# Column sums by zero-and-one matrices in a hybrid decoder layer: fp32 products replaced by pairs of fp32r products

## Chip, cores and metric

One core of one Trainium2 chip. The metric is the device time of one execution in microseconds; given are the median of three runs and one profiled execution, from which all views of the trace come. Engines: PE is TensorE (PEld its weight load), DVE is VectorE, ACT is ScalarE, POOL is GpSimd, SP is the engine that issues most DMAs.

## What is computed

A decoder layer over 2048 tokens and 1024 columns. The input projection feeds two mixers that run side by side: four HGRN2 heads of 128 columns and eight RWKV-7 heads of 64 columns. The output projection, a feed-forward block with a causal convolution, and a last norm follow. Cut to what matters here:

```python
h = _rmsnorm(x, norm1_w[l]);  proj = h @ w_in[l]
# HGRN2: o from a gated recurrence, then a norm over the 128 columns of a head
o = o * lax.rsqrt(jnp.mean(o * o, axis=-1, keepdims=True) + NORM_EPS)
# RWKV-7, heads of 64 columns
kk = heads(k * k_k)
kk = kk / jnp.maximum(jnp.sqrt(jnp.sum(kk * kk, axis=-1, keepdims=True)), L2_EPS)
y = _rwkv7_scan(heads(r), heads(decay), heads(k), heads(v), -kk, kk * heads(a))
var = jnp.mean(jnp.square(y - mu), axis=-1, keepdims=True)
y = ((y - mu) * lax.rsqrt(var + RW_GN_EPS)).reshape(B, T, RW_WIDTH)
bonus = jnp.sum(heads(r * k * r_k), axis=-1, keepdims=True) * heads(v)
```

The four sums over a head's columns (of `o * o`, `kk * kk`, `(y - mu)^2` and `r * k * r_k`) are what the change touches.

## The kernel before

Activations stand with their columns on the 128 partitions and 512 tokens (a block) on the free axis. A sum over the columns of a head is then a sum over partitions, and the kernel makes it on PE with a 128x128 matrix of zeros and ones: `ones`, all ones, for a head of 128 columns; `blk1`, two 64x64 squares of ones, for a pair of 64-column heads. Each such product also spreads the sum over the head's partitions.

The first stage (`phase1`, until about 1430 us) runs three generators. `dense` makes the projections: it loads a slice of weights, splits it into two fp32r halves (an ACT cast into `wh`, line 243, and a DVE subtraction of the cast from the source into `wl`, line 244), and makes every product as three fp32r products (`mm3`, lines 259 to 261), accumulated in the banks `pj`. Behind the columns of a block it turns the next block's rows (`turn`, line 427: transposes by `ident`, evicted by ACT into `xt`). `rw_super` treats four RWKV heads (two pairs, `u` = 0 and 1) of one block: eight runs of it. `hg_unit` treats one HGRN2 head of one block: sixteen runs. Each `yield` ends a step; a driver takes one step of each mixer and then fills 2 us of estimated TensorE time with projection work. Each engine runs its instructions in the order in which the scheduler put them, so that order is fixed before the kernel runs.

Four places make the sums, all as plain fp32 products. In `rw_super`: line 648 sums `sq`, a part of the tile `mk` (the squared keys); line 666 sums `BV` (r * k * r_k); line 886 sums `y1`, a part of `yo` (the squared outputs). Each makes two products of 128x512, one for each pair. In `hg_unit`, line 1016 sums `osq` in one product. The trace shows each product as two records. In the texts these are the sums of mk, of BV, of yo and of hg. The end of one `rw_super` (yo) and the beginning of the next (mk, BV, then the arrays AR and KB, and the first products of the chunk, line 687) stand close together; this stretch is called a boundary. Line 1022 and line 901 store the mixers' outputs, and the second stage begins with the last block's output projection.

The tiles with the tags `E` and `Ti` hold a triangular inverse (lines 749 to 767), solved by DVE in the middle of a run; before the solve, lines 750 and 751 clear `Ti` and set its diagonal.

Of the kernel before, what the change touches and what calls it, by code (L numbers as in the profile page):

```python
# [7 lines left out]
F32 = mybir.dt.float32  # L8
F32R = mybir.dt.float32r
# [3 lines left out]
ALU = mybir.AluOpType  # L13
# [5 lines left out]
P = 128  # L19
# [3 lines left out]
BLK = 512  # L23
# [6 lines left out]

C_CEN, C_ONE, C_S1, C_DG = 0, 128, 256, 384
C_LV = 448
C_SCAN = C_LV + 6 * 64
C_ID = C_SCAN + 512
C_W = C_ID + 128
# [26 lines left out]
def tile_layer(ctx, tc, consts, x, norm1_w, w_in, hg_lb_logits, hg_norm_w, rw_shift_mu, rw_w0, rw_w2,  # L62
# [17 lines left out]
    ident = cp.tile([P, P], F32, name="ident")  # L80
    cst = cp.tile([P, C_ID], F32, name="cst")
    dma(ident, consts[:, C_ID:C_ID + P])
# [3 lines left out]
    cen = cst[:, C_CEN:C_CEN + P]  # L86
    blk1 = cst[:, C_ONE:C_ONE + P]
    s1m = cst[:, C_S1:C_S1 + P]
    dgm = cst[:, C_DG:C_DG + 64]
    scanm = cst[:, C_SCAN:C_SCAN + 512]  # L90
    ones = cp.tile([P, P], F32, name="ones")
    V.memset(ones, 1.0)

# [3 lines left out]
    def eps_tile(v, name):  # L97
        t_ = cp.tile([P, 1], F32, name=name)
        V.memset(t_, v)
        return t_  # L100

    eps6 = eps_tile(1e-6, "eps6")
    epsgn = eps_tile(64e-5, "epsgn")

    tables = {AF.Exp: "natural_log_exp_and_others", AF.Ln: "natural_log_exp_and_others",
# [48 lines left out]
    def vec(nm, i):  # L154
        return vt[:, off[nm] + i:off[nm] + i + 1]
# [4 lines left out]
    lb1 = vt[:, off["lb"] + 4:off["lb"] + 8]  # L160
    ltmp = cp.tile([P, 16], F32, name="ltmp")
    V.tensor_max(ltmp[:, 0:4], lb0, lb1)
# [9 lines left out]
    V.tensor_scalar(omu, vt[:, off["mu"]:off["mu"] + 14], -1.0, 1.0, ALU.mult, ALU.add)  # L172
    oka = cp.tile([P, 16], F32, name="oka")[:, 0:4]
    V.tensor_scalar(oka, vt[:, off["ka"]:off["ka"] + 4], -1.0, 1.0, ALU.mult, ALU.add)
# [60 lines left out]
    def split_to(hi, lo, src):  # L235
        S.copy(hi, src)
        V.tensor_sub(lo, src, hi.bitcast(F32))
# [9 lines left out]
    def transposed(xt, nm, psum, evict):  # L247

        n = len(xt)
        for k in range(KD):  # L250
# [4 lines left out]
            yield 109 * n  # L255

    def mm3(acc, lhs, rhs, first, last, skip=False):
        (lh, ll), (rh, rl) = lhs, rhs
        TE.matmul(acc, lh, rh, start=first, stop=False, skip_group_check=skip)  # L259
        TE.matmul(acc, lh, rl, start=False, stop=False, skip_group_check=skip)  # L260
        TE.matmul(acc, ll, rh, start=False, stop=last, skip_group_check=skip)  # L261

    def phase1(c1):
# [7 lines left out]
        g2 = hp.tile([P, 512], F32, name="g2")  # L271
        lastc = hp.tile([P, 64], F32, name="lastc")
        nc.gpsimd.memset(lastc, 0.0)
        Xc = hp.tile([P, 4, 64], F32, name="Xc")
        nc.gpsimd.memset(Xc, 0.0)
# [205 lines left out]
        def constants():  # L481

            dma(w2a2[0:64, :], rw_w2[0])
            dma(w2a2[64:128, :], rw_a2[0])
            dma(cst, consts[:, 0:C_ID])
            dma(g2, rw_g2[0])
# [121 lines left out]
        U = range(2)  # L608

        def rw_super(nb, s_):  # L610
# [6 lines left out]
            def tile_(tag, shape, name):  # L617
                return rp.tile([P] + shape, F32, tag=tag, name=name)

            def bank2():  # L620
                return ps.tile([P, 2, BLK], F32, tag="rw", name="rw", bufs=2)
# [12 lines left out]
            mk_ = tile_("M", [4, 2, BLK], "mk")  # L634
            c, km, sq = mk_[:, 0], mk_[:, 1], mk_[:, 2]
            for u in U:
                V.tensor_tensor_scan(c[:, u], scanm, iW[:, u], 0.0, ALU.mult, ALU.add)
                act(sq[:, u], k[:, u], AF.Square, scale=vec("kk", prs[u]))
                act(km[:, u], a[:, u], AF.Identity, bias=oka[:, prs[u]:prs[u] + 1], scale=vec("ka", prs[u]))
            yield  # L640
            W = tile_("UV", [16, 65], "W")
            WC = tile_("WC", [16, 1], "WC")
            V.memset(W[:, :, 0:1], 1.0)
            act(W[:, :, 1:65], c16(c), AF.Exp, scale=NEG_C)
            act(iW, c, AF.Exp, scale=-NEG_C)
            b1 = bank2()
            for u in U:
                TE.matmul(b1[:, u, :], blk1, sq[:, u], start=True, stop=True)
            V.tensor_scalar_max(sq, b1, 1e-24)
# [9 lines left out]
            V.tensor_mul(RT, r4(r), W4[:, :, :, 1:65])  # L659
            yield  # L660
            BV = tile_("BV", [2, BLK], "BV")
            b1 = bank2()
            for u in U:
                V.scalar_tensor_tensor(BV[:, u], km[:, u], vec("rk", prs[u]), r[:, u], ALU.mult, ALU.mult)
            for u in U:
                TE.matmul(b1[:, u, :], blk1, BV[:, u], start=True, stop=True)
            for u in U:
# [213 lines left out]
            y1, y2 = yo[:, 0], yo[:, 1]  # L881
            act(y1, yp, AF.Square)
            yield
            b1 = bank2()
            for u in U:
                TE.matmul(b1[:, u, :], blk1, y1[:, u], start=True, stop=True)
            act(y1, b1, AF.Ln, bias=epsgn, scale=1.0 / 64)
# [18 lines left out]
        def hg_unit(nb, j):  # L906
# [105 lines left out]
            sq = rp.tile([P, BLK], F32, tag="hk", name="osq")  # L1012
            act(sq, op, AF.Square)
            yield
            ms = bank("hg")
            TE.matmul(ms, ones, sq, start=True, stop=True)
            act(sq, ms, AF.Ln, bias=eps6, scale=1.0 / 128)
# [471 lines left out]
```

## Time and profile before

| what | value |
|---|---|
| three runs, median (lowest to highest) | 2788.16 us (2784.22 to 2788.61) |
| profiled execution | 2785.02 us |
| its span, first to last instruction | 2783.2 us |
| mean granted TensorE clock | 0.984 |
| PE, DVE, ACT busy | 2678.8, 2066.4, 1421.1 us |
| DMA moved | 435.01 MB, mean 156 GB/s |

A row of a group names line, engine, operation, what it writes and reads, the shape and the count; then busy time and the mean of one in ns; then the idle time of the engine before it and what ended most of it. A row in order of time gives start, length and in brackets the idle time before. Matmuls are pipelined and their ends are modelled, so the records of neighbouring matmuls overlap: what one costs is seen from the distance of the starts.

### The profile page before, as it was taken

The numbers are of one execution on the slowest core, as the hardware profiler recorded it, in microseconds if no ns is written. First come the engines' busy times: TensorE is split into PE (matmuls) and PEld (weight loads), VectorE is DVE, ScalarE is ACT, GpSimd is POOL, SyncE is SP. The second block draws the span as 40 slices with busy tenths as digits, with TensorE's granted clock in tenths as the row PEclk, the third lists the DMA queues.
The fourth block names the chain that finished last, engine by engine and source line by source line (L and its number), as shares of the span: only waits on it lengthen the run. The fifth ranks groups of instructions, "written<-read, shape, count | busy, mean of one in ns | idle before, by whom it ended". The sixth has DMA issues, their size and how long they took to land.

```text
span 2783.2 us, 47784 instructions
## 1 busy us (share of the span) xinstructions
PE 2678.8 (96%) x18059; PEld 2135.2 (77%) x18059; DVE 2066.4 (74%) x3877; ACT 1421.1 (51%) x2254; POOL 11.1 (0%) x24
## 2 busy tenths in 40 slices
PE   8999999989999999999989999998999999999998
PEld 6877777767787777777767888886888888877887
DVE  4867778685686766868658789989997877677656
ACT  5445454544646446435346765456455555445444
POOL 0000000000000000000000000000000000000000
PEclk9999999999999999999899999999999999999999
DMA  5222322244441344543475457756672223998855
GB/s 163 72 69 72 99 73 78 63 131 141 131 121 58 102 141 136 161 132 94 131 239 178 143 172 262 239 165 216 205 245 88 87 76 135 324 333 310 289 193 186
DMA packets 429628, 435.01 MB, mean 156 GB/s; under 512 B 68703, under 2 KB 288213, under 8 KB 429397
## 3 DMA queue, kind: packets, MB, share of 16 engines
q1 hardware_dynamic: 428337, 429.30, 48.4%
q8 instruction: 142, 2.33, 0.3%
q0 software_dynamic: 992, 2.64, 0.2%
q14 instruction: 89, 0.73, 0.1%
q10 hardware_dynamic: 68, 0.02, 0.0%
HBM read 325.94 MB, written 105.91 MB: 155 GB/s over the span
## 4 chain that ended last, share of the span: by engine, by line
PE 78%; DVE 7%; ACT 7%; DMA 4%; issue 3%; SPq 1%; DVEq 0%; ACTq 0%
PE pj L259 8%; PE pj L260 8%; PE pj L261 8%; PE ua L261 6%; PE ua L259 5%; PE ua L260 5%; PE ud L259 3%; PE ud L260 3%; PE ud L261 3%; PE da L260 2%; PE da L261 2%; PE da L259 2%; PE hg L948 2%; PE db L259 2%; PE db L260 2%
## 5 line engine op out<-in xcount | busy, mean ns | idle before, releaser
L259 PE MATMUL pj<-hh,wh 128*128 128x512 f32 x960 | 401.8, 419 | 0.9 <-DVE xh L398 0.4
L260 PE MATMUL pj<-hl,wh 128*128 128x512 f32 x960 | 379.9, 396 | 0.0
L261 PE MATMUL pj<-hh,wl 128*128 128x512 f32 x960 | 379.0, 395 | 0.2 <-DVE wl L244 0.2
L243 ACT CAST wh<-wraw 128x512 fp32r<-128x512 f32 x240 | 147.0, 619 | 307.9 <-PE pj L260 266.2
L259 PE MATMUL ua<-Bh,uwh 128*128 128x512 f32 x704 | 278.6, 396 | 15.0 <-ACT uwh L243 13.7
L261 PE MATMUL ua<-Bh,uwl 128*128 128x512 f32 x704 | 276.6, 393 | 0.7 <-DVE uwl L244 0.7
L260 PE MATMUL ua<-Bl,uwh 128*128 128x512 f32 x704 | 276.5, 393 | 0.0
L244 DVE TENSOR_TENSOR wl<-wraw,wh 128x512 fp32r<-128x512 f32 x240 | 163.3, 686 | 133.8 <-ACT wh L243 132.9
L259 PEld LDWEIGHTS pj<-hh,wh 128*128 128x128 f32 x960 | 180.8, 188 | 53.1 <-issue 13.6
L260 PEld LDWEIGHTS pj<-hl,wh 128*128 128x128 f32 x960 | 180.9, 188 | 42.4 <-issue 7.9
L243 ACT CAST uwh<-uraw 128x512 fp32r<-128x512 f32 x220 | 134.9, 618 | 151.2 <-PE ua L260 80.0
L261 PEld LDWEIGHTS pj<-hh,wl 128*128 128x128 f32 x960 | 180.7, 188 | 39.9 <-issue 1.3
L243 ACT CAST dah<-draw 128x512 fp32r<-128x512 f32 x151 | 93.8, 621 | 182.7 <-PE da L260 50.5
L244 DVE TENSOR_TENSOR uwl<-uraw,uwh 128x512 fp32r<-128x512 f32 x220 | 146.9, 685 | 50.8 <-ACT uwh L243 50.8
L244 DVE TENSOR_TENSOR dal<-draw,dah 128x512 fp32r<-128x512 f32 x151 | 104.2, 690 | 107.0 <-ACT dah L243 106.8
L259 PEld LDWEIGHTS ua<-Bh,uwh 128*128 128x128 f32 x704 | 133.5, 190 | 44.0 <-ACT uwh L243 14.3
L261 PEld LDWEIGHTS ua<-Bh,uwl 128*128 128x128 f32 x704 | 133.6, 190 | 30.4 <-DVE uwl L244 2.3
L260 PEld LDWEIGHTS ua<-Bl,uwh 128*128 128x128 f32 x704 | 133.6, 190 | 27.2
L259 PE MATMUL ud<-Bh,uwh 128*128 128x512 f32 x352 | 137.9, 392 | 1.9 <-DVE cv L1340 1.9
L261 PE MATMUL ud<-Bh,uwl 128*128 128x512 f32 x352 | 137.1, 389 | 0.0
L260 PE MATMUL ud<-Bl,uwh 128*128 128x512 f32 x352 | 137.0, 389 | 0.0
L260 PE MATMUL da<-dbl,dah 128*128 128x512 f32 x340 | 133.5, 393 | 1.7 <-DVE dbl L244 1.6
(314 smaller groups left out, 5959.7 us busy)
## 6 DMA issues: line engine op xcount, KB each, us to landing
wraw<-in_w_in_dram SPq DMA_DIRECT2D x240, 256.0 KB, 3.0
uraw<-in_w_up_dram SPq DMA_DIRECT2D x176, 256.0 KB, 3.3
woraw<-in_w_out_dram SPq DMA_DIRECT2D x96, 256.0 KB, 3.1
draw<-Sg SPq DMA_DIRECT2D x88, 256.0 KB, 2.9
draw<-Tw SPq DMA_DIRECT2D x88, 256.0 KB, 3.0
gd<-y SPq DMA_DIRECT2D x86, 256.0 KB, 2.9
xt<-x1d SPq DMA_DIRECT2D x32, 512.0 KB, 6.6
draw<-gd SPq DMA_DIRECT2D x63, 256.0 KB, 5.1
```

The lines of the kernel that those rows point to most:

```text
L243: S.copy(hi, src)
L244: V.tensor_sub(lo, src, hi.bitcast(F32))
L259: TE.matmul(acc, lh, rh, start=first, stop=False, skip_group_check=skip)
L260: TE.matmul(acc, lh, rl, start=False, stop=False, skip_group_check=skip)
L261: TE.matmul(acc, ll, rh, start=False, stop=last, skip_group_check=skip)
L948: TE.matmul(o, kt[:, t0:t0 + 64], qs, start=True, stop=True, tile_position=(0, e * 64))
```

## The change

Every one of these fp32 products becomes two fp32r products. The source is split as the weights are: ACT casts it into an upper half (`hi`), DVE subtracts the cast from the source into a lower half (`lo`), and PE multiplies the zero-and-one matrix with each half and accumulates both in the same bank. The matrix itself becomes an fp32r tile. In `rw_super` both pairs are split by one cast and one subtraction of 1024 columns, one step before the products, so the four products of a sum stand together; the halves lie in the memory of the tags `E` and `Ti`. For that, the two DVE products that make `BV` move ahead of a `yield`. In `hg_unit` the halves are two tiles of the ring `hX`. `blk1` is loaded by a DMA of its own and cast by DVE; `ones` is made from `ident` by one DVE instruction. Some small tiles change their size or place.

```diff
-    blk1 = cst[:, C_ONE:C_ONE + P]
-    ones = cp.tile([P, P], F32, name="ones")
-    V.memset(ones, 1.0)
+    blk1, ones = (cp.tile([P, P], F32R, name=n_) for n_ in ("blk1", "ones"))
+    V.tensor_scalar(ones, ident, 0.0, 1.0, ALU.mult, ALU.add)
...
+    def mm_sum(accs, mat, his, los):
+        for acc, hi, lo in zip(accs, his, los):
+            TE.matmul(acc, mat, hi, start=True, stop=False)
+            TE.matmul(acc, mat, lo, start=False, stop=True)
...
-            dma(cst, consts[:, 0:C_ID])
+            dma(cst, consts[:, 0:C_ONE])
+            raw = wp.tile([P, P], F32, tag="wraw", name="blk", bufs=4)
+            dma(raw, consts[:, C_ONE:C_ONE + P])
+            V.tensor_copy(blk1, raw)
...
             c, km, sq = mk_[:, 0], mk_[:, 1], mk_[:, 2]
+            hi, lo = (rp.tile([P, 2, BLK], F32R, tag=t_, name="hl") for t_ in ("E", "Ti"))
             for u in U:
...
+            split_to(hi, lo, sq)
             yield
...
-            for u in U:
-                TE.matmul(b1[:, u, :], blk1, sq[:, u], start=True, stop=True)
+            mm_sum([b1[:, u, :] for u in U], blk1, [hi[:, u] for u in U], [lo[:, u] for u in U])
             V.tensor_scalar_max(sq, b1, 1e-24)
...
             V.tensor_mul(RT, r4(r), W4[:, :, :, 1:65])
-            yield
             BV = tile_("BV", [2, BLK], "BV")
+            for u in U:
+                V.scalar_tensor_tensor(BV[:, u], km[:, u], vec("rk", prs[u]), r[:, u], ALU.mult, ALU.mult)
+            split_to(hi, lo, BV)
+            yield
             b1 = bank2()
-            for u in U:
-                V.scalar_tensor_tensor(BV[:, u], km[:, u], vec("rk", prs[u]), r[:, u], ALU.mult, ALU.mult)
-            for u in U:
-                TE.matmul(b1[:, u, :], blk1, BV[:, u], start=True, stop=True)
+            mm_sum([b1[:, u, :] for u in U], blk1, [hi[:, u] for u in U], [lo[:, u] for u in U])
...
             act(y1, yp, AF.Square)
+            hi, lo = (rp.tile([P, 2, BLK], F32R, tag=t_, name="hl") for t_ in ("E", "Ti"))
+            split_to(hi, lo, y1)
             yield
             b1 = bank2()
-            for u in U:
-                TE.matmul(b1[:, u, :], blk1, y1[:, u], start=True, stop=True)
+            mm_sum([b1[:, u, :] for u in U], blk1, [hi[:, u] for u in U], [lo[:, u] for u in U])
...
             act(sq, op, AF.Square)
+            osp = [rp.tile([P, BLK], F32R, tag="hX", name="osp", bufs=3) for _ in range(2)]
+            split_to(*osp, sq)
             yield
             ms = bank("hg")
-            TE.matmul(ms, ones, sq, start=True, stop=True)
+            mm_sum([ms], ones, osp[:1], osp[1:])
```

Two places in the order of the instructions follow. Line numbers of the changed kernel are higher: its lines 236 and 237 are the cast and the subtraction of a split, 260 and 261 the two products of a sum, 265 to 267 the three products of a projection.

First boundary without transposes, PE around the sum of BV (`hl` is a half, `blk_76` the matrix), before:

```order
L261 MATMUL pj<-hh,wl 128x512
L666 MATMUL rw<-BV,cst 128x512 x2
L259 MATMUL pj<-hh,wh 128x512
L260 MATMUL pj<-hl,wh 128x512
L261 MATMUL pj<-hh,wl 128x512
```

and now:

```order
L267 MATMUL pj<-hh,wl 128x512
L260 MATMUL rw<-hl,blk_76 128x512
L265 MATMUL pj<-hh,wh 128x512
L266 MATMUL pj<-hl,wh 128x512
L267 MATMUL pj<-hh,wl 128x512
L265 MATMUL pj<-hh,wh 128x512
L261 MATMUL rw<-hl,blk_76 128x512
L260 MATMUL rw<-hl,blk_76 128x512
L261 MATMUL rw<-hl,blk_76 128x512
```

Between the sum of mk and that of BV stood 18 products of the projection; now 33 stand ahead of the first product of BV's upper half, and four more ahead of the lower half's. DVE at the same boundary, before, from BV on:

```order
L664 SCALAR_TENSOR_TENSOR BV<-mk,vt,rkv_358 128x512 x2
L654 COPY WC<-W 128x16
L659 TENSOR_TENSOR AR<-rkv_358,W 128x2x512
L649 TENSOR_SCALAR mk<-rw 128x1024
L672 TENSOR_TENSOR KB<-mk,ai 128x8x2x64
L333 SCALAR_TENSOR_TENSOR hq<-pj,sgm 128x512
L244 TENSOR_TENSOR wl<-wraw,wh 128x512 x2
L674 TENSOR_TENSOR ai<-ai 128x1024
```

and now:

```order
L672 SCALAR_TENSOR_TENSOR BV<-mk,vt,rkv_363 128x512 x2
L659 TENSOR_SCALAR mk<-rw 128x1024
L664 COPY WC<-W 128x16
L669 TENSOR_TENSOR AR<-rkv_363,W 128x2x512
L682 TENSOR_TENSOR KB<-mk,ai 128x8x2x64
L340 SCALAR_TENSOR_TENSOR hq<-pj,sgm 128x512
L244 TENSOR_TENSOR wl<-wraw,wh 128x512 x2
L684 TENSOR_TENSOR ai<-ai 128x1024
L237 TENSOR_TENSOR hl<-BV,hl 128x1024
L678 SCALAR_TENSOR_TENSOR mk<-rkv_446,vt,mk 128x512 x2
```

BV is made at the same place; its lower half stands eight instructions behind it.

First boundary with transposes, ACT (`xt` are the evictions of the transposes), before:

```order
L117 ACTIVATE hf<-pj 128x512
L113 ACT_TABLE_LOAD
L117 ACTIVATE mk<-mk 128x1024
L117 ACTIVATE xt<-pj 128x4x128
L117 ACTIVATE mk<-mk 128x1024
L117 ACTIVATE xt<-pj 128x4x128 x2
L243 CAST wh<-wraw 128x512
```

and now:

```order
L118 ACTIVATE hf<-pj 128x512
L114 ACT_TABLE_LOAD
L118 ACTIVATE mk<-mk 128x1024
L236 CAST hl<-BV 128x1024
L118 ACTIVATE mk<-mk 128x1024
L118 ACTIVATE xt<-pj 128x4x128 x2
L243 CAST wh<-wraw 128x512
```

The cast of BV stands ahead of the first eviction, which itself moved behind the second mk row.

More of the change, by code (lines that the diff above doesn't have):

```diff
@@ L29 @@
 HG_SCALE = 128.0 ** -0.5
-C_CEN, C_ONE, C_S1, C_DG = 0, 128, 256, 384
-C_LV = 448
+C_CEN, C_S1, C_DG = 0, 128, 256
+C_LV = 320
 C_SCAN = C_LV + 6 * 64
-C_ID = C_SCAN + 512
+C_ONE = C_SCAN + 512
+C_ID = C_ONE + 128
 C_W = C_ID + 128
@@ L80, in tile_layer @@
     ident = cp.tile([P, P], F32, name="ident")
-    cst = cp.tile([P, C_ID], F32, name="cst")
+    cst = cp.tile([P, C_ONE], F32, name="cst")
     dma(ident, consts[:, C_ID:C_ID + P])
@@ L103, in tile_layer @@
     epsgn = eps_tile(64e-5, "epsgn")
+    ltmp = cp.tile([P, 16], F32, name="ltmp")
+    blk1, ones = (cp.tile([P, P], F32R, name=n_) for n_ in ("blk1", "ones"))
+    V.tensor_scalar(ones, ident, 0.0, 1.0, ALU.mult, ALU.add)
     tables = {AF.Exp: "natural_log_exp_and_others", AF.Ln: "natural_log_exp_and_others",
@@ L160, in tile_layer @@
     lb1 = vt[:, off["lb"] + 4:off["lb"] + 8]
-    ltmp = cp.tile([P, 16], F32, name="ltmp")
     V.tensor_max(ltmp[:, 0:4], lb0, lb1)
@@ L172, in tile_layer @@
     V.tensor_scalar(omu, vt[:, off["mu"]:off["mu"] + 14], -1.0, 1.0, ALU.mult, ALU.add)
-    oka = cp.tile([P, 16], F32, name="oka")[:, 0:4]
+    oka = cp.tile([P, 32], F32, name="oka")[:, 0:4]
     V.tensor_scalar(oka, vt[:, off["ka"]:off["ka"] + 4], -1.0, 1.0, ALU.mult, ALU.add)
@@ L271, in phase1 @@
         g2 = hp.tile([P, 512], F32, name="g2")
-        lastc = hp.tile([P, 64], F32, name="lastc")
+        lastc, WC = (hp.tile([P, 32], F32, name=n_) for n_ in ("lastc", "WC"))
         nc.gpsimd.memset(lastc, 0.0)
+        WC = WC[:, 0:16].unsqueeze(2)
         Xc = hp.tile([P, 4, 64], F32, name="Xc")
@@ L639, in rw_super @@
                 act(km[:, u], a[:, u], AF.Identity, bias=oka[:, prs[u]:prs[u] + 1], scale=vec("ka", prs[u]))
+            split_to(hi, lo, sq)
             yield
             W = tile_("UV", [16, 65], "W")
-            WC = tile_("WC", [16, 1], "WC")
             V.memset(W[:, :, 0:1], 1.0)
@@ L659, in rw_super @@
             V.tensor_mul(RT, r4(r), W4[:, :, :, 1:65])
-            yield
             BV = tile_("BV", [2, BLK], "BV")
-            b1 = bank2()
             for u in U:
                 V.scalar_tensor_tensor(BV[:, u], km[:, u], vec("rk", prs[u]), r[:, u], ALU.mult, ALU.mult)
-            for u in U:
-                TE.matmul(b1[:, u, :], blk1, BV[:, u], start=True, stop=True)
+            split_to(hi, lo, BV)
+            yield
+            b1 = bank2()
+            mm_sum([b1[:, u, :] for u in U], blk1, [hi[:, u] for u in U], [lo[:, u] for u in U])
             for u in U:
```

## Prediction

> **What bounds the kernel now.** I read the busy shares first, then the chain of work that ended last.
>
> ```profile
> PE 2678.8 (96%) x18059; PEld 2135.2 (77%) x18059; DVE 2066.4 (74%) x3877; ACT 1421.1 (51%) x2254; POOL 11.1 (0%) x24
> ...
> PE 78%; DVE 7%; ACT 7%; DMA 4%; issue 3%; SPq 1%; DVEq 0%; ACTq 0%
> ```
>
> TensorE is busy 96% of the span and makes 78% of the chain, so a microsecond of matmul is worth up to a microsecond. The average hides stages; the windows show them (length, PE busy, PEld, DVE, ACT, POOL, granted clock, DMA share, GB/s).
>
> ```profile
> 200.00:300.00 100.00, 95.01 (x640) 72.14 (x639) 78.70 (x170) 58.31 (x85) 0.00 (x0) 1.00 0.27 77
> 600.00:700.00 100.00, 91.02 (x944) 67.95 (x945) 64.22 (x141) 41.31 (x66) 0.00 (x0) 0.95 0.51 156
> 1300.00:1430.00 130.00, 115.10 (x1110) 89.65 (x1107) 83.85 (x200) 48.64 (x82) 1.80 (x3) 0.87 0.44 138
> 1500.00:2000.00 500.00, 487.14 (x2154) 399.35 (x2153) 440.57 (x680) 290.24 (x448) 0.00 (x0) 0.99 0.59 193
> ```
>
> All sums lie before 1430 us, where the mixers run; what follows is untouched. There PE is nearly full in most windows, and lets go where an output projection runs (600 to 700, 1300 to 1430), with a lower clock.
>
> **What is removed and added on PE.** The four lines of sums, two records for each 128x512 product, so 16 products a line, 64 in all:
>
> ```profile
> L648 PE MATMUL rw<-mk,cst x32: 591/592/595, 68.2 to 1257.8; 128*128 128x512 f32 x32
> L666 PE MATMUL rw<-BV,cst x32: 591/592/697, 74.0 to 1263.6; 128*128 128x512 f32 x32
> L886 PE MATMUL rw<-yo,cst x32: 591/592/593, 202.6 to 1408.1; 128*128 128x512 f32 x32
> L1016 PE MATMUL hg<-osq,ones x32: 590/592/1220, 139.4 to 1404.3; 128*128 128x512 f32 x32
> ```
>
> Durations overlap, so prices come from starts. PE in order of time around the first two products:
>
> ```profile
> 67.52 0.39 PE L259 MATMUL pj<-hh,wh 128*128 128x512 f32 x1
> 67.75 0.39 PE L260 MATMUL pj<-hl,wh 128*128 128x512 f32 x1
> 67.97 0.39 PE L261 MATMUL pj<-hh,wl 128*128 128x512 f32 x1
> 68.20 1.88 PE L648 MATMUL rw<-mk,cst 128*128 128x512 f32 x4
> 69.51 0.79 PE L259 MATMUL pj<-hh,wh 128*128 128x512 f32 x1
> 70.15 0.39 PE L260 MATMUL pj<-hl,wh 128*128 128x512 f32 x1
> ```
>
> A short-format product starts every 0.227 us (0.68 from 67.52 to 68.20, by three). From 68.20 to 70.15 are 1.95 us; less one short product that is 1.72 for two sums, 0.86 each. A sum now becomes two short products, 0.455. The saving is 0.405 a sum, 64 x 0.405 = 25.9 us: 13.0 for the 32 sums of mk and BV, 6.5 for yo, 6.5 for the hg units. [...]
>
> **What is added on ACT and DVE.** The nearest rows for a cast and a subtraction, of 512 and of 1024 columns:
>
> ```profile
> L243 ACT CAST wh<-wraw 128x512 fp32r<-128x512 f32 x240 | 147.0, 619 | 307.9 <-PE pj L260 266.2 <-DMA wraw<-in_w_in_dram 19.7 <-issue 11.7
> L244 DVE TENSOR_TENSOR wl<-wraw,wh 128x512 fp32r<-128x512 f32 x240 | 163.3, 686 | 133.8 <-ACT wh L243 132.9
> L117 ACT ACTIVATE mk<-mk 128x1024 f32<-128x1024 f32 x16 | 16.9, 1055 | 0.1
> L1366 DVE TENSOR_TENSOR y<-y,y 128x1024 f32<-128x1024 f32 x44 | 53.9, 1224 | 0.0
> ```
>
> 24 pair splits and 16 single ones: ACT 24 x 1.06 + 16 x 0.62 = 35 us, DVE 24 x 1.22 + 16 x 0.69 = 40 us. Both engines have that much idle time before 1430 us, so the total costs nothing; its place does. A sum now starts 1.06 + 1.22 = 2.28 us (hg: 1.31) after its source unless PE has other matmuls standing ahead of it. Uncovered everywhere that would be 24 x 2.28 + 16 x 1.31 = 76 us; covered everywhere 0. I go place by place.
>
> *yo and hg.* The first such place:
>
> ```profile
> 198.78 1.02 ACT L117 ACTIVATE yo<-rw 128x1024 f32<-128x1024 f32 x1 [2.32 <-PE rw L878]
> 200.75 0.60 ACT L117 ACTIVATE osq<-hg 128x512 f32<-128x512 f32 x1 [0.95 <-PE hg L1011]
> 202.62 1.88 PE L886 MATMUL rw<-yo,cst 128*128 128x512 f32 x4
> 204.34 1.02 PE L1016 MATMUL hg<-osq,ones 128*128 128x512 f32 x2
> ```
>
> The square ends at 199.8; plus 2.28 is 202.1, before PE gets there at 202.62. For osq: yo's cast to 200.9, osq to 201.5, its cast to 202.1, its subtraction to 202.8; PE needs it at 202.62 + 0.91 = 203.5. Covered; for the rest I take 1.0 us over all 24 sites, near the lower of 0 and (8 x 2.28 + 16 x 1.31) 39.
>
> *mk and BV, five boundaries without the block's transposes.* mk's source is early and its sums keep their place. BV is different, by the new DVE order: the lower half stands behind eight instructions, the last of which (ai) ends in the rows of before at 77.1, and its cast stands behind the first of ACT's two mk rows.
>
> ```profile
> 69.25 1.41 DVE L664 SCALAR_TENSOR_TENSOR BV<-mk,vt,rkv 128x512 f32<-128x512 f32 x2
> 75.86 1.22 DVE L674 TENSOR_TENSOR ai<-ai 128x1024 f32<-128x1024 f32 x1
> 75.52 1.06 ACT L117 ACTIVATE mk<-mk 128x1024 f32<-128x1024 f32 x1
> 83.75 1.16 PE L687 MATMUL rw<-AR,KB 64*128 64x128 f32 x16 [0.53 <-DVE KB L675]
> ```
>
> Cast from 76.5 to 77.6, lower half at 78.8. PE: mk's products end at 68.20 + 0.91 = 69.1; 37 short products and BV's first stand ahead of the lower half: 38 x 0.227 = 8.6, so PE is there at 77.7 and waits 1.1 us. Behind it in PE's queue stand the projection's matmuls, and behind the subtraction in DVE's the chain to KB, on which L687 already waits 0.53; I leave that as it is. Bounds 0 and 2.28, taken 1.1: 5 x 1.1 = +5.5. The clear of Ti (0.91 us) moves here from free time, since its memory now holds lower halves; the matmuls that DVE feeds afterwards stand behind projection work, so nothing; uncovered it is 8 x 0.9 = 7.
>
> *mk and BV, three boundaries with transposes, one for each block but the first.*
>
> ```profile
> 213.01 1.27 ACT L117 ACTIVATE ai<-rw,vt 128x512 f32<-128x512 f32 x2 [1.91 <-PE rw L629]
> ...
> 222.00:232.00 10.00, 6.58 (x38) 4.18 (x37) 10.00 (x12) 9.93 (x15) 0.00 (x0) 1.00 0.18 49
> ...
> 231.83 0.66 PE L427 MATMUL pj<-ident,xt 128*128 128x128 f32 x4 [1.25 <-ACT xt L117]
> ...
> 232.52 0.60 ACT L117 ACTIVATE xt<-pj 128x512 f32<-128x512 f32 x1 [0.26 <-PE pj L427]
> ```
>
> ACT and DVE are full for ten microseconds, PE idles a third of it waiting for ACT's evictions. BV's cast (1.06) joins that queue; yo's and mk's casts (2.12) go into ACT's 1.91 us of idle time before the boundary, but for 0.2: the last eviction is 1.3 us later. Nothing saved on PE counts here: 3 x (4 x 0.405 + 1.3) = +8.8, between 3 x 1.62 = 4.9 (cover) and 3 x (1.62 + 2 x 2.28) = 18.5.
>
> *Projections and the end.* Where PE is not the bound the saving goes into its idle time: four sums, +1.6 (0 to 4). The last yo of the mixers:
>
> ```profile
> 1405.04 1.03 ACT L117 ACTIVATE yo<-rw 128x1024 f32<-128x1024 f32 x1
> ...
> 1406.82 1.88 PE L886 MATMUL rw<-yo,cst 128*128 128x512 f32 x4
> ```
>
> Its sums start at 1406.1 + 2.28 = 1408.4, 1.6 later, and take 0.8 less: +0.8. The new load of the block matrix and the moved constants lie in the start, ahead of their first use at 68 us: 0 (a late one at most 1).
>
> Sum: -25.9 + 1.0 + 5.5 + 8.8 + 1.6 + 0.8 = -8.2 us. The profiled execution took 2785.0 (span 2783.2, and 1.8 around it that nothing here touches); the median shown is 3.1 higher. So 2776.8 for such an execution, 2780 as a median.
>
> **The rivals.** *Covered after all* (chance 0.28): the new order sets the boundary matmuls later, and only the end, the small waits and the projections cost: -25.9 + 3.4 = -22.5, 2766. For it: PE at 95% and more in most windows. Against it: ACT and DVE both full at 222.
>
> *Another stretch at half clock* (0.12). TensorE lost its clock once like this:
>
> ```profile
> 1352.12 0.88 PE L990 MATMUL hg<-ident,hk 128*128 128x128 f32 x3 [2.95 <-DVE hk L983]
> ...
> 1350.00:1360.00 10.00, 7.88 (x63) 6.88 (x64) 4.16 (x12) 2.78 (x6) 0.00 (x0) 0.50 0.21 66
> 1360.00:1370.00 10.00, 10.00 (x103) 7.60 (x104) 3.57 (x7) 3.71 (x8) 0.00 (x0) 0.50 0.31 96
> 1370.00:1380.00 10.00, 7.90 (x230) 7.42 (x228) 5.20 (x10) 6.17 (x12) 0.00 (x0) 0.84 0.45 145
> ```
>
> After 2.95 us idle the clock was 0.50: 5.0 + 5.0 + 1.6 = 11.6 us lost. If a later split lengthens one stall of a projection as far, -8.2 + 11.6 = +3.4, 2792. Against it: the long waits of boundaries are broken up by transposes. [...]
>
> *The splits choke ACT and DVE at every boundary* (0.16), slower: all eight behave like the three, 8 x 2.9 = 23.4 in place of 5.5 + 8.8, and half of yo's and hg's 13.0 goes to weight casts that queue behind splits, 6.5: -8.2 + 9.1 + 6.5 = +7.4, 2796. It decides from 25.9 / 40 = 0.65 us of exposed wait per split. For it: DVE 10.00 of 10. Against: 200 to 300 has DVE at 79%.
>
> *The change doesn't do what it says* (0.02): the new products cost what the old did, and the splits come on top: -8.2 + 25.9 = +17.7, 2806.
>
> **How the numbers follow.** The forecast has 0.42, its own range 2773 to 2787. This kernel's runs tell 0.2% (5.6 us) from no change. Of the forecast's 0.42, 0.27 is faster and 0.15 the same; the covered case is faster; of the half clock 0.03 the same and 0.09 slower; the rest slower. Faster 0.55, same 0.18, slower 0.27. The range 2762 to 2798 reaches over the covered case and the choked one.
>
> **What would show it.** The sums' products start 0.23 us apart; PE waits about 1 us for the lower half of BV at the first boundary, and the last eviction at the first transposes comes 1 to 2 us later against the work around it; yo's and hg's products wait for nothing. Waits of over 2 us at BV or waits at yo would prove the price too low, a granted clock under 1 in new windows the second rival; a BV that waits for nothing, the first.

## The result and the profile after

The changed kernel takes 2790.0 us (median of 13 runs, 2786.12 to 2796.63), the kernel before 2784.22 (13 runs, 2777.91 to 2788.61): a ratio of 1.0024, 95% interval 1.0015 to 1.0033. It is slower by 6.7 us (4.2 to 9.2), where 2780 was forecast. The profiled execution took 2791.68 us, its span is 2789.8.

The busy shares and the chain of the changed kernel:

```profile
PE 2671.8 (96%) x18059; PEld 2139.9 (77%) x18059; DVE 2101.1 (75%) x3918; ACT 1448.9 (52%) x2294; POOL 11.1 (0%) x24
...
PE 29%; DVE 3%; DMA 2%; issue 1%; ACT 1%; SPq 0%; DVEq 0%; ACTq 0%
```

The splits themselves take 40 us of DVE and 35 of ACT, as costed; the totals of these engines rise by less, 34.7 and 27.8 us. PE's busy time, in which records at half clock count with their full length, is only 7 us lower. The chain here could be followed for little more than a third of the span, so its 29% says nothing against the 78% of before.

The same windows as before (length, PE busy, PEld, DVE, ACT, POOL, granted clock, DMA share, GB/s):

```profile
200.00:300.00 100.00, 93.47 (x628) 72.92 (x628) 82.21 (x175) 60.68 (x88) 0.00 (x0) 0.97 0.28 82
600.00:700.00 100.00, 94.17 (x931) 70.12 (x932) 63.76 (x135) 43.82 (x70) 0.00 (x0) 0.95 0.54 168
1300.00:1430.00 130.00, 112.67 (x1146) 88.07 (x1145) 86.51 (x209) 50.36 (x84) 1.79 (x3) 0.90 0.44 132
1500.00:2000.00 500.00, 483.49 (x2128) 394.99 (x2127) 434.18 (x671) 285.24 (x443) 0.00 (x0) 0.98 0.59 190
```

PE is idle longer from 200 to 300 and its clock fell there from 1.00 to 0.97. Summed over the 10-us windows from 60 to 1420 us, PE stands idle for 65.2 us (before 54.4), and the busy time times what the granted clock lacks to 1 is 35.4 us (before 25.0). So in these two executions some 21 us came back as waits (10.8) and as a lower clock (10.4), of the 25.9 taken out of PE's work. The part of the clock is likely smaller as a rule: the profiled execution's mean granted clock, 0.978, is at the lower end of the 13 (median 0.981, before 0.984).

The mixers end (first product of the last output projection) at 1428.5 us, before at 1425.5; the rest takes 1361.4, before 1357.7, with no instruction in another order. This second difference is spread between executions and not the change: in the traces of the runs below, which all have the changed memory, the rest takes from 1357.6 us (bvlate) to 1363.1 (layout, which as a whole is level with before).

The products of a sum, PE in order of time at the first boundary:

```profile
64.71 0.39 PE L267 MATMUL pj<-hh,wl 128*128 128x512 f32 x1
64.93 0.39 PE L260 MATMUL rw<-hl,blk 128*128 128x512 f32 x1
65.16 0.39 PE L261 MATMUL rw<-hl,blk 128*128 128x512 f32 x1
65.39 0.39 PE L260 MATMUL rw<-hl,blk 128*128 128x512 f32 x1
65.61 0.39 PE L261 MATMUL rw<-hl,blk 128*128 128x512 f32 x1
65.84 0.39 PE L265 MATMUL pj<-hh,wh 128*128 128x512 f32 x1
```

They start 0.227 us apart, 0.91 for four where two long ones took 1.72. The waits for BV in this boundary, and then at the first transposes:

```profile
74.31 0.50 PE L260 MATMUL rw<-hl,blk 128*128 128x512 f32 x1 [0.83 <-ACT hl L236]
...
221.94 0.80 PE L260 MATMUL rw<-hl,blk 128*128 128x512 f32 x1 [2.65 <-ACT hl L236]
223.41 0.79 PE L261 MATMUL rw<-hl,blk 128*128 128x512 f32 x1 [0.67 <-DVE hl L237]
...
220.00:230.00 10.00, 7.33 (x32) 5.70 (x33) 9.33 (x13) 8.10 (x12) 0.00 (x0) 0.66 0.17 49
520.00:530.00 10.00, 7.67 (x28) 5.96 (x27) 10.00 (x15) 8.49 (x11) 0.00 (x0) 0.66 0.07 21
```

At 74 us the wait has about the forecast size (1.1), but PE waits for BV's upper half; the lower one, of which the forecast was made, is there in time. At 222 PE waits 2.65 us for BV's upper half with the transposes standing behind it in its queue, and the clock is 0.66, where it was 1.00 before. Not all of this fall is the split's: run layout below has no split and the order of before, and in its trace the clock of the first of these windows is 0.83:

```profile
220.00:230.00 10.00, 7.41 (x37) 4.97 (x36) 10.00 (x14) 9.47 (x14) 0.00 (x0) 0.83 0.19 52
```

And DVE, the groups of the new subtractions (count, busy time and mean in ns, idle time before them):

```profile
L237 DVE TENSOR_TENSOR osp<-osq,osp 128x512 fp32r<-128x512 f32 x16 | 11.0, 687 | 6.5 <-ACT osp L236 6.5
...
L237 DVE TENSOR_TENSOR hl<-mk,hl 128x1024 fp32r<-128x1024 f32 x8 | 9.8, 1225 | 2.9 <-ACT hl L236 2.9
L237 DVE TENSOR_TENSOR hl<-yo,hl 128x1024 fp32r<-128x1024 f32 x8 | 9.8, 1225 | 9.9 <-ACT hl L236 9.9
L237 DVE TENSOR_TENSOR hl<-BV,hl 128x1024 fp32r<-128x1024 f32 x8 | 9.8, 1221 | 1.4 <-ACT hl L236 1.4
```

Beside 40 us of work, DVE stands 20.7 us in its queue waiting for casts, most of it at yo and hg. Of these the forecast had said that they wait for nothing, and there it looked only at PE. For PE it is nearly so: in this trace PE's idle time right ahead of the products of yo and hg is 1.4 us in all, and by the distances of the starts PE loses some 5 us there at most (an estimate). Ahead of BV's products its idle time is 7.7 us, 5.4 of it at the first and third boundary with transposes.

### The profile page after: what moved, and what is told of

It reads as the page before. It is cut to its first block, busy times and chain, and to the rows that moved or that the text cites. A ratio compares the mean times of both kernels' runs of the same rounds, so it can differ in the third digit from the quotient of the medians.

```text
span 2789.8 us, 47865 instructions
## 1 busy us (share of the span) xinstructions
PE 2671.8 (96%) x18059; PEld 2139.9 (77%) x18059; DVE 2101.1 (75%) x3918; ACT 1448.9 (52%) x2294; POOL 11.1 (0%) x24
## 3 DMA queue, kind: packets, MB, share of 16 engines
q0 software_dynamic: 992, 2.64, 0.2%
## 5 line engine op out<-in xcount | busy, mean ns | idle before, releaser
L265 PE MATMUL pj<-hh,wh 128*128 128x512 f32 x960 | 391.4, 408 | 4.0 <-ACT xt L118 1.7
```

## The experiments

Ratios are against runs of the kernel before on the same chip; 0.001 is 2.8 us. "Short" means that a sum is made of fp32r products.

| run | what differs | median us | ratio | 95% interval |
|---|---|---|---|---|
| layout | all sums long; memory as changed | 2783.12 | 0.9998 | 0.9989 to 1.0006 |
| hg | hg short | 2789.07 | 1.0019 | 1.0007 to 1.0031 |
| yohg | yo, hg short | 2787.51 | 1.0014 | 1.0004 to 1.0024 |
| nobv | mk, yo, hg short | 2783.23 | 0.9993 | 0.9979 to 1.0007 |
| (changed) | all short | 2790.0 | 1.0024 | 1.0015 to 1.0033 |
| mkyo | mk, yo short | 2782.09 | 0.9997 | 0.9987 to 1.0007 |
| hgdead | hg long, its splits made but unread | 2789.94 | 1.0024 | 1.0012 to 1.0035 |
| hgcast | hg long, its casts made but unread | 2783.48 | 1.0004 | 0.9994 to 1.0014 |
| hgsub | hg long, a dead subtraction, no cast | 2796.39 | 1.0043 | 1.0029 to 1.0056 |
| hghi | hg short, upper half only | 2782.82 | 0.9999 | 0.9988 to 1.0010 |
| hgpool | hg short, lower half by GpSimd | 2794.80 | 1.0046 | 1.0034 to 1.0058 |
| nobvpool | nobv, hg's lower half by GpSimd | 2788.61 | 1.0021 | 1.0009 to 1.0033 |
| bvlate | changed, BV's products two steps later | 2790.56 | 1.0027 | 1.0016 to 1.0038 |
| bvhi | changed, BV with the upper half only | 2784.72 | 1.0003 | 0.9993 to 1.0013 |
| memp | layout, clears on GpSimd | 2786.44 | 1.0001 | 0.9990 to 1.0013 |
| mkyomemp | mkyo, clears on GpSimd | 2783.92 | 0.9998 | 0.9985 to 1.0010 |
| aftermemp | changed, clears on GpSimd | 2789.50 | 1.0007 | 0.9996 to 1.0018 |
| allhi | all short, upper halves only | 2777.88 | 0.9968 | 0.9954 to 0.9981 |
| direct | allhi, casts left out too | 2767.02 | 0.9936 | 0.9924 to 0.9948 |

**Which sum loses?** Four kernels undo the change in parts. Where a sum is long again, its product reads the fp32r matrix bit for bit as fp32:

```diff
-            split_to(hi, lo, sq)
...
-            mm_sum([b1[:, u, :] for u in U], blk1, [hi[:, u] for u in U], [lo[:, u] for u in U])
+            for u in U:
+                TE.matmul(b1[:, u, :], blk1.bitcast(F32), sq[:, u], start=True, stop=True)
```

Run layout:

> All 64 sums are long-format products again, in their old places, without splits; what stays of the change is the memory: the block matrix and the ones in tiles of their own, the constants moved, the block matrix's own load and copy, the smaller tiles. Placement theory (the 3.7 us that the changed kernel loses after 1428 us, where no instruction differs, come from where tiles and constants lie): 3 to 5 us slower than before. Boundary theory (all of the loss comes from the splits among the transposes) and choke theory (from the splits everywhere): as before, within 1.5 us, and the stage behind the mixers takes about 1358 us as before.

Run hg:

> The layout of the change, and only the 16 sums of the hg units as short products with their splits; mk, BV and yo as before. Forecast's price: 16 x 0.405 = 6.5 us off, so 6 us faster than before if the splits are covered and the layout costs nothing. Choke theory: weight casts queue behind the 16 splits, gain 3 us or less. Placement theory: 3 to 4 us less gain than that, about 2 us faster.

Run yohg:

> The sums of yo and hg as short products, mk and BV as before, in their old places. Boundary theory: 13 us of TensorE work gone and nothing among the transposes, so 9 to 13 us faster than before. Choke theory: at most 5 us faster. Placement theory: 6 to 9 us faster. The granted clock between 220 and 230 us is 1.00 as before by the boundary theory.

Run nobv:

> As the changed kernel, but BV's sums are long-format products again in their old place, with no split in the boundary behind the mk sums. Boundary theory (BV's split stands among the transposes in TensorE's queue, TensorE waits 2.7 us and loses its clock): the clock at 220 to 230 us is back at 1.00, and the kernel is 12 to 19 us faster than the changed one, that is 7 to 13 us faster than before. Choke theory: still slower than or level with before, since mk's, yo's and hg's splits stay. Placement theory: 3 to 4 us of the changed kernel's loss stay.

Layout is level: the placement theory falls. The surprise is hg: 16 sums that should have given 6.5 us cost 5.3. From run to run the steps are hg +5.8 (against layout), yo -1.4, mk -5.8, BV +8.6, each to about 4 us either way. A step holds only on top of the ones ahead of it: run mkyo below has mk's and yo's sums short without hg's, and they don't give the 7.2 us there. The boundary theory has half of it: taking BV out does bring 8.6 us back, but the kernel without it is only level with before, and its clock from 220 to 230 us is 0.83, not the 1.00 that this theory expected.

**What of a split costs?** The hg sums are the cleanest place, with nothing else moved by hand. Four variants of run hg's split:

```diff
# hgpool
-            split_to(*osp, sq)
+            S.copy(osp[0], sq)
+            nc.gpsimd.tensor_sub(osp[1], sq, osp[0].bitcast(F32))
# hgdead: splits stay
-            mm_sum([ms], ones, osp[:1], osp[1:])
+            TE.matmul(ms, ones.bitcast(F32), sq, start=True, stop=True)
# hgcast: the same product, and
-            split_to(*osp, sq)
+            S.copy(osp, sq)
# hghi: that cast, and
+            TE.matmul(ms, ones, osp, start=True, stop=True)
```

Run hgpool:

> Only the hg sums short, as in run hg, but their lower halves are made by GpSimd instead of VectorE. VectorE theory (run hg lost 5 us against before, not TensorE time: near 1178 us VectorE waits 1.15 us for the cast and works 0.6 on the lower half in the middle of the triangular solve, and TensorE, whose projection work is gated there, waits for what follows the solve): the loss goes, 4 to 7 us faster than before. Order theory (the scheduler's other order of some 400 TensorE and VectorE instructions costs the 5 us): about as run hg, 3 to 7 us slower than before. Latency theory (the sums' own chain is 1 to 2 us longer in each unit): as run hg or slower, since GpSimd is not faster.

Run nobvpool, the same edit on nobv:

> As run nobv (mk, yo and hg short, BV in the long format), with the lower halves of hg made by GpSimd. VectorE theory: the 10 us between run hg's forecast and result come back in part, so 6 to 12 us faster than run nobv, 8 to 13 us faster than before. Order and latency theories: as run nobv, about level with before.

Run hgdead:

> As run hg, with the same casts and subtractions, but the hg sums are long-format products of the unsplit squares, as before; the halves are read by nobody. VectorE theory: slower than before by at least as much as run hg (5 us), and up to the 6.5 us of TensorE time more, 5 to 12 us. Latency theory (the products wait for the halves): level with before, since no product waits for a split. Forecast's price (splits covered): level with before, within 1.5 us.

Run hgcast:

> As run hgdead, without the subtraction: the hg sums are long-format products of the unsplit squares, and beside them stand 16 casts that nobody reads. VectorE theory: level with before, within 2 us. Cast theory: 3 to 6 us slower than before, as run hgdead. Order theory: not level with before, most likely slower.

Run hghi:

> Only the hg sums short, and only with the upper half: the lower halves, their subtractions on VectorE and their products are left out (the sums lose the digits below the cast). VectorE theory (8 of the 16 subtractions fall into the triangular solves, each of which ran 0.8 us longer in run hg and run hgdead, and what follows a solve waits for it): with no subtraction left the 5 us of run hg go, 2 to 10 us faster than before. Cast theory (ScalarE's 16 casts, or the square's place in the chain, cost it): as run hg, 3 to 6 us slower than before. Order theory (any other order of the instructions costs it): also 3 to 6 us slower.

Hgcast is level (1.0004): what the 16 casts cost, if anything, doesn't show (interval -1.7 to +3.9 us). Hgdead adds the 16 subtractions to it, 11 us of DVE, and is 5.6 us slower than hgcast (1.0024 and 1.0004): the loss is there although no product reads a half, so no product's wait for its split makes it. And PE's time brings little here: hg against hgdead saves 6.5 us of PE and gains 1.4, hghi against hgcast saves 16 x 0.63 = 10.1 and gains 1.4, each to about 4 us either way. (The second pair isn't clean: hghi has an order on ACT, shown below, that hgcast lacks and that costs it some 5 us of its trace.) The latency theory falls. Hghi was also to be 2 to 10 us faster than before by the VectorE theory; it was level.

GpSimd is no way out: its subtractions in the profile of hgpool (duration in ns, least, median, most), and PE waiting for one:

```profile
L1025 POOL TENSOR_TENSOR osp<-osq,osp x16: 1268/1354/2928, 136.7 to 1375.1; 128x512 fp32r<-128x512 f32 x16
...
298.48 0.80 PE L261 MATMUL hg<-osp,ones 128*128 128x512 f32 x1 [1.99 <-POOL osp L1025]
```

1354 ns where DVE takes 687. PE then waits for the halves, 1.99 us in this row. Nor does DVE get all of its time back: this step of the solve, which runs at the same time as GpSimd's subtraction, takes 1.39 us, where the same step takes 0.30 in run hg (hgpool's two rows, then hg's):

```profile
1186.08 1.45 POOL L1025 TENSOR_TENSOR osp<-osq,osp 128x512 fp32r<-128x512 f32 x1 [138.13 <-PE pj L266]
1186.31 1.39 DVE L768 TENSOR_TENSOR Ti<-Ti,etmp 64x156 f32<-64x156 f32 x1
...
1179.76 0.30 DVE L768 TENSOR_TENSOR Ti<-Ti,etmp 64x156 f32<-64x156 f32 x1
```

Hgpool and nobvpool are 12.8 and 5.8 us slower than before. Both miss what the VectorE theory expected, and neither is a clean test of it, since a step of DVE's solve got longer instead (the 1.39 us above).

**Where the subtraction bites.** DVE in order of time in the profile of hgdead, in the middle of a triangular solve (etmp and Ti):

```profile
1180.06 0.69 DVE L237 TENSOR_TENSOR osp<-osq,osp 128x512 fp32r<-128x512 f32 x1 [1.15 <-ACT osp L236]
1180.66 0.30 DVE L766 TENSOR_TENSOR etmp<-E,Ti 64x156 f32<-64x156 f32 x1
```

DVE runs the solve and what is put between its steps, and here it waits 1.15 us and works 0.6 on the subtraction. This solve lasts 46.0 us, in hgcast 44.8. 8 of the 16 subtractions fall into the eight solves; together the solves last 339.6 us in hgdead, 335.7 in hgcast and 333.2 in layout. What follows a solve stands on the chain through `rw_super`, and there the traces differ most. In hgcast, ACT and PE a little later (line 795 multiplies the solved inverse, ACT evicts the product into TZ, line 809 needs that; Af belongs to the hg unit):

```profile
1205.51 1.20 ACT L118 ACTIVATE TZ<-rw 32x512 f32<-32x512 f32 x2 [0.92 <-PE rw L795]
1206.74 0.84 ACT L118 ACTIVATE Af<-A 64x256 f32<-64x256 f32 x2
...
1204.79 0.69 PE L795 MATMUL rw<-TZ,M 32*32 32x32 f32 x30
1206.15 0.24 PE L809 MATMUL rw<-TTs,TZ 32*32 32x32 f32 x2 [0.68 <-ACT TZ L118]
...
1210.00:1220.00 10.00, 9.25 (x231) 8.04 (x232) 7.58 (x11) 4.97 (x9) 0.00 (x0) 0.83 0.73 234
```

and in hgdead:

```profile
1213.44 0.84 ACT L118 ACTIVATE Af<-A 64x256 f32<-64x256 f32 x2 [2.28 <-DVE A L963]
1214.31 1.20 ACT L118 ACTIVATE TZ<-rw 32x512 f32<-32x512 f32 x2
...
1210.96 0.69 PE L795 MATMUL rw<-TZ,M 32*32 32x32 f32 x32
1214.95 0.31 PE L809 MATMUL rw<-TTs,TZ 32*32 32x32 f32 x2 [3.30 <-ACT TZ L118]
...
1210.00:1220.00 10.00, 6.40 (x121) 4.27 (x122) 7.63 (x18) 5.78 (x11) 0.00 (x0) 0.66 0.17 61
```

The scheduler put Af ahead of TZ on ACT. Af waits for DVE, TZ stands behind it, PE waits 3.30 us in place of 0.68, and the granted clock is 0.66. (The windows cut these stretches: the whole one at half clock is 10.2 us long in hgdead, from 1213.3, and 6.8 in hgcast, from 1206.5.) In the changed kernel it is the same:

```profile
1208.30 0.84 ACT L118 ACTIVATE Af<-A 64x256 f32<-64x256 f32 x2 [2.28 <-DVE A L965]
1209.17 1.20 ACT L118 ACTIVATE TZ<-rw 32x512 f32<-32x512 f32 x2
...
1209.81 0.31 PE L810 MATMUL rw<-TTs,TZ 32*32 32x32 f32 x2 [3.30 <-ACT TZ L118]
```

How much goes there is seen from the starts of the state products (hg<-VT,KT) of the hg units 13 and 14, on either side of this place:

| runs | unit 1 to 13 | unit 13 to 14 |
|---|---|---|
| before, layout, hgcast (TZ first) | 1039.4, 1041.5, 1039.9 | 65.0, 66.1, 66.2 |
| memp, mkyo (Af first) | 1042.8, 1037.0 | 68.6, 68.4 |
| hg, hgdead, hgsub, changed (Af first) | 1043.3, 1044.0, 1042.5, 1040.8 | 70.1, 71.2, 70.6, 70.8 |
| hghi, allhi, direct (Af first) | 1036.3, 1035.2, 1032.8 | 71.1, 73.5, 69.5 |

Times are in us, each from one execution; before and layout, which have the same order, show how far two executions differ. (The other eight kernels have Af first too, with 68.4 to 71.6. In mkyo, hghi, allhi and direct only the first of the two Af stands ahead of TZ.) PE runs the same 126 products of the projection between the two units in every kernel, and yet every kernel in which Af stands first takes 2 to 7 us longer than layout here, also those that add nothing to DVE. In their traces two waits of PE are longer. One is the wait for TZ: 2.45 to 3.31 us in place of 0.68. The other, in most of them but not in memp, mkyo and direct, comes some 20 us earlier, where an hg unit waits for DVE; in hgdead it is

```profile
1194.45 0.69 PE L957 MATMUL hg<-hq,hk 128*64 128x64 f32 x16 [2.25 <-DVE hk L918]
```

The two executions of hgdead and hgcast differ by 11.3 us (by the ratios it is 5.6): 5.0 lie between units 13 and 14, and 4.1 in the 1040 us ahead of them. That this swap on ACT by itself costs these microseconds was not tried: no run has the splits and the old order. A changed order as such need not cost anything, for memp has DVE's and PE's instructions in another order than layout as well and is level.

**BV.** Two variants of the changed kernel:

```diff
# bvlate: BV's products are written two steps later
-            b1 = bank2()
-            mm_sum([b1[:, u, :] for u in U], blk1, [hi[:, u] for u in U], [lo[:, u] for u in U])
...
+            b1 = bank2()
+            mm_sum([b1[:, u, :] for u in U], blk1, [hi[:, u] for u in U], [lo[:, u] for u in U])
             V.tensor_mul(BV, b1, v)
# bvhi: upper half only
-            split_to(hi, lo, BV)
+            S.copy(hi, BV)
```

Run bvlate:

> The changed kernel, but BV's four products stand two steps later, right ahead of their reader; the split stays where it is. Queue theory (TensorE stands at BV's products among the transposes, waits for the halves, and the clock falls): the clock at 220 and 520 us is back near 1.00, 4 to 8 us faster than the changed kernel. Engine theory (ACT and DVE lack the time for the extra cast and subtraction in the boundary, wherever the products stand): no more than 2 us faster than the changed kernel.

Run bvhi:

> The changed kernel, but BV's sums take the upper half alone: BV's subtraction on VectorE and the lower products are left out, its cast on ScalarE stays. VectorE theory (the subtraction of 1.22 us in the boundary, where VectorE is full, costs the 7 us between the changed kernel and run nobv): 5 to 9 us faster than the changed kernel, at or below run nobv. Cast theory (the cast of 1.03 us ahead of the evictions of the transposes costs it): at most 3 us faster than the changed kernel.

PE and the clock at the first transposes in bvlate, then in bvhi:

```profile
223.59 0.50 PE L260 MATMUL rw<-hl,blk 128*128 128x512 f32 x1 [2.65 <-ACT hl L236]
```

```profile
222.33 1.22 PE L677 MATMUL rw<-hl,blk 128*128 128x512 f32 x2 [2.64 <-ACT hl L673]
...
220.00:230.00 10.00, 6.75 (x28) 4.94 (x28) 9.85 (x15) 9.29 (x15) 0.00 (x0) 0.66 0.18 52
520.00:530.00 10.00, 7.53 (x26) 5.85 (x26) 9.85 (x16) 8.41 (x12) 0.00 (x0) 0.66 0.00 1
```

Bvlate is no test of the queue: the scheduler put the products back to the same place among the transposes, with the same wait. Bvhi is one, for the clock: wait and clock are those of the changed kernel (2.64 us, 0.66 and 0.66), and yet it is 5.8 us faster. So the new half-clock stretch at the transposes is not what BV costs most: 5.8 of its 8.6 us go with its subtraction of 1.22 us and the 16 lower products (3.6 us of PE).

**Is it DVE's time as such?**

```diff
-            V.memset(Sf, 1.0)
+            nc.gpsimd.memset(Sf, 1.0)
...
-            V.memset(Ti[0:n], 0.0)
+            nc.gpsimd.memset(Ti[0:n], 0.0)
```

and the same for Ti's diagonal. Run memp:

> As run layout (all sums in the long format, no splits), but three clears (the 512 columns of Sf in each hg unit, 0.485 us, 16 times; Ti's 0.912 and its diagonal's 0.085, 8 times) run on GpSimd instead of VectorE: 15.8 us less for VectorE, nothing else changed. VectorE theory (in the mixers a microsecond of VectorE is worth about half a microsecond of the end, as hgdead against hgcast has it): 4 to 8 us faster than before. TensorE theory (the forecast's: the mixers are bound by TensorE): level with before, within 1.5 us.

Run aftermemp:

> The changed kernel with the clears on GpSimd. In it the clear of Ti stands in the boundary. VectorE theory: 5 to 9 us faster than the changed kernel, level with before or a little faster. TensorE theory: as the changed kernel.

Run hgsub, a subtraction that waits for no cast (`V.tensor_sub(osp, sq, sq)` in place of hgcast's cast):

> As run hgcast, but the dead instruction is a VectorE subtraction of the square from itself in place of the cast: it has the length of a split's subtraction (0.69 us), but waits for the square alone and not for a cast. Work theory (16 more VectorE instructions at that place of its queue cost the 5.5 us between hgdead and hgcast): 4 to 6 us slower than before. Wait theory (VectorE standing in its queue for the cast, 1.15 us in the middle of a solve, costs them): within 2 us of before.

Memp is level: 15.8 us of clears taken from DVE (its busy time falls by 10.9 us against layout) bring nothing, and the theory that DVE's time bounds the mixers falls in that general form. (Memp has Af first as well, and its loss of 2.5 us there may hide as much of a gain.) Hgsub is 10.9 us slower than hgcast: the loss needs no cast, only 16 more instructions of 0.69 us in DVE's queue. Whether it is their work or the wait ahead of them stays open, for DVE stands in its queue here too, waiting for the square: 7.4 us over the 16, in hgdead 5.7 for the cast. One of these waits, again inside a solve:

```profile
1176.76 0.69 DVE L1024 TENSOR_TENSOR osp<-osq 128x512 fp32r<-128x512 f32 x1 [1.40 <-ACT osq L118]
```

(Why hgsub is 5.3 us worse than hgdead stays open; its profiled execution was among its fastest.) Aftermemp lies 4.7 us below the changed kernel, but the intervals overlap, so it decides nothing.

**Parts put together, and what is left to have.** Run mkyo:

> Only the sums of mk and yo as short products, hg and BV as before. If the parts add up as the runs so far have them (yo 1.5 us and mk 4.3 us faster, by the differences of runs yohg, hg and nobv): 2778 to 2780, 5 to 6 us faster than before. Forecast's price: 13 us of TensorE time less, 8 to 12 us faster. Choke theory (any split costs more than its products give): no faster than before.

Run mkyomemp:

> As run mkyo (mk and yo short), with the clears on GpSimd. VectorE theory: 20 us of subtractions added and 15.8 us of clears taken away, 13 us of TensorE saved: 4 to 8 us faster than run mkyo, 5 to 10 us faster than before. TensorE theory: as run mkyo, 1 to 2 us faster than before.

Run allhi (every lower half, its subtraction and its product left out):

> All 64 sums short with the upper halves alone: the lower halves, their subtractions (40 us of VectorE) and their products are left out, the casts stay; TensorE is spared 64 x 0.63 = 40 us against before. Forecast's price of TensorE time: 25 to 38 us faster than before. VectorE theory (TensorE's saved time ends as waits where the mixers' chains decide, as run hghi was level with before for 10 us saved): at most 8 us faster than before.

Run direct:

```diff
-                act(sq[:, u], k[:, u], AF.Square, scale=vec("kk", prs[u]))
+                act(hi[:, u], k[:, u], AF.Square, scale=vec("kk", prs[u]))
...
-            act(sq, op, AF.Square)
+            act(osp, op, AF.Square)
```

and in the same way for yo and BV.

> As run allhi, without the casts too: ScalarE's squares of mk, yo and hg and VectorE's product BV are written as fp32r at once, so that the 64 short products come with no instruction added to any engine; the lower halves are left out, and the sums lose the digits below the rounding. If casts are free, as run hgcast has it: as run allhi, 8 to 10 us faster than before. If the casts ahead of the evictions at the boundaries cost what is left: 12 to 20 us faster than before. TensorE theory: 25 us or more.

Mkyo and mkyomemp, the parts that looked good, are level: 13 us of PE, and nothing to be seen of it in the time (mkyo -0.8, interval -3.6 to +1.9). Allhi and direct give the change's account. Direct spares PE 64 x 0.63 = 40 us and adds no instruction: 17.8 us faster. The casts take 8.9 of it back (allhi), the subtractions and lower products another 15.6 (the changed kernel): -17.8 + 8.9 + 15.6 = +6.7. Casts do cost, then, though at hg none of it shows; at which of the other sums was not tried. Direct is the fastest kernel of the study, 18 us below before and 24 below the changed one; its sums lack what the lower halves add, so it is to be had only where that is allowed.

## Why the prediction was wrong

**The step that failed** is the paragraph on yo and hg: "Covered; for the rest I take 1.0 us over all 24 sites". It gave -13.0 + 1.0 = -12.0 us; run yohg measured +3.9 (interval 1.1 to 6.7). It is 15.9 us too low, and the whole gap between the sum (-8.2) and the result (+6.7) is 14.9; the other terms nearly cancel. As a wait of PE the 1.0 was not far off (1.4 us of idle time in the trace, some 5 at most); wrong was that this wait is the price. Two assumptions stand in it.

First, a split was priced by how long PE waits at its own product; the runs show that the subtraction costs with no product behind it (hgdead against hgcast, 5.6 us; hgsub). "Both engines have that much idle time before 1430 us, so the total costs nothing; its place does" agrees with memp, but the place was then only looked at from PE, and the subtraction stands in DVE's queue, in half of the hg units inside a solve. By which road it then costs the 5.6 us is not shown: the traces have longer solves, a wait for DVE in the hg units and the swap on ACT, and no run tells these apart.

Second, "a microsecond of matmul is worth up to a microsecond" was taken at its upper end in the stages where PE is 95% busy: direct, which adds no instruction, has 40 us worth 17.8, and hghi has 10.1 worth 1.4.

**PE's products**: 0.227 us apart, the saving of a sum as forecast.

**mk and BV**: forecast -13.0 + 5.5 + 8.8 = +1.3, measured -5.8 for mk and +8.6 for BV, +2.8. The sum came out, in part by luck: mk's gain is not seen in mkyo, where hg's sums are long. At the five boundaries without transposes PE's idle time ahead of BV's products is 2.4 us in all, where 5.5 was taken; at the first it is 0.83, and for the other half than forecast. Among the transposes, PE's wait for BV (2.65) and the clock (0.66) were not foreseen, but bvhi shows that they decide little.

**Layout and load**: 0 forecast, -0.6 measured (interval -3.1 to +1.7). **Projections and end**, +1.6 and +0.8: too small for any run here to show.

**The rivals.** *Another stretch at half clock* came nearest in time (2792): the clock did fall in new windows (0.66 at 220 and at 520 us), and the account above has 10 us of it in one execution; but bvhi keeps the fall at the transposes and loses nothing against before, and the fall at 1210 us comes with a wait on ACT's order (3.30 us), not with the lengthened projection stall that the rival named. *The splits choke* (2796) named the right sums, yo's and hg's, but half of their gain, 6.5 us, where 15.9 went, and the wrong road: weight casts behind splits, where hgcast, with the casts at hg, is level (1.0004). *Covered after all* fell, and so did *The change doesn't do what it says*, by the products 0.227 us apart. What no rival had is that the saved PE time itself is worth less than half.

## What to carry over

A busy share of 96% is not a price: before a saving on the fullest engine is counted, one kernel that drops the work outright (as hghi and direct do) gives a bound on what the saving is worth. Price an added instruction by its own engine's queue and by the chain that passes through it, not by the wait of the reader it serves. And where a scheduler sets the order, an edit can reorder far places, as on ACT at 1205 us here, so look at the one or two places where the traces part before blaming the edit.

## What the runs showed of the hardware

Two executions with the same order of instructions differ by 4.4 us at one place. Before, at the 2.95 us wait that ends at 1352 us, had a clock of 0.50, 0.50 and 0.84 in three 10-us windows (its rows are in the prediction); layout, at a wait of 2.94 us there, had

```profile
1352.31 0.88 PE L999 MATMUL hg<-ident,hk 128*128 128x128 f32 x3 [2.94 <-DVE hk L992]
...
1350.00:1360.00 10.00, 7.69 (x68) 6.60 (x68) 4.34 (x13) 2.84 (x6) 0.00 (x0) 0.66 0.14 44
1360.00:1370.00 10.00, 9.27 (x240) 7.70 (x244) 3.71 (x8) 8.02 (x16) 0.00 (x0) 1.00 0.53 175
1370.00:1380.00 10.00, 8.63 (x190) 7.76 (x180) 6.17 (x13) 2.57 (x7) 0.00 (x0) 0.83 0.44 133
```

From unit 16 to the mixers' end that is 66.5 us in layout and 70.9 before. In before the clock fell at 1349.5 us, 0.3 us into the wait and not after all of it, as the prediction has it, and stayed at 0.5 for 20.5 us; in layout it was at 0.5 for 6.8 us between 1350 and 1360 (0.66 over that window, 1.00 in the two beside it). How long it stayed low at the same wait was thus not fixed by the order of the instructions, and one trace prices this stall no better than to the 4.4 us between the two. In the traces of before and of the changed kernel the granted clock is either 1 or 0.5, and but for the last stretch of each trace every stretch at 0.5 lasts a multiple of 3.41 us (3.4, 6.8, 10.2, 13.7, 17.1 or 20.5). In the other 18, what the 10-us windows lack to 1 adds up, for each group of neighbouring windows that begins and ends between 60 and 1430 us, to 3.4 to 20.4 us at 0.5, within 0.2 us of such multiples.
